# Tile start addresses of a one-core transformer block rearranged to multiples of 128 bytes in SBUF

## The chip, the cores and the metric

The program runs on one core of one Trainium2 chip. The metric is the device time of one execution in microseconds (us); several runs of each kernel are taken and the median is given. The profile is one further execution, recorded by the hardware profiler. The core's engines are TensorE (PE, with its weight loads listed apart as PEld), VectorE (DVE), ScalarE (ACT), GpSimd (POOL) and SyncE (SP, which issues the DMAs). All compute engines work on SBUF, 128 partitions of which each holds a row of every tile; a tile's start is a byte address that is the same in every partition. Matmul results go to PSUM.

## The reference, cut to what matters

The computation is one transformer block on 512 tokens of width 1024, in float32: a gated three-branch attention (compressed, selected and window keys) and a spatial gating unit side by side, then a feed-forward layer with a short convolution.

```
h = rms_norm(x, attn_norm);  proj = h @ w_in
q, kc, vc, ks, vs, kw, vw, gl, uv = split(proj)
o_nsa = nsa(q, compress(kc), compress(vc), ks, vs, kw, vw, sigmoid(gl), rel_bias)
o_sgu = u * (tril(sgu_w) @ rms_norm(v) + sgu_b)      # u, v = halves of gelu(uv)
x = x + concat([o_nsa, o_sgu]) @ w_out
up = rms_norm(x, ffn_norm) @ w_up                    # 1024 -> 2 * 2816
up = causal_conv3(up) + conv_b;  a, g = halves(up)
x = x + (silu(g) * a) @ w_down                       # 2816 -> 1024
```

## The kernel before, in words

**Precision.** Nearly every product is made of three matmuls. Each float32 operand is split into a high part in TensorE's float32r type and the remainder, also in float32r, and `mm3` (line 245) adds high by high, high by low and low by high into one PSUM bank. In `mm3` the argument `st` is the stationary operand (loaded as weights), `mv` the moving one that streams through:

```
TE.matmul(out, st[0], mv[0], start=first, stop=False)
TE.matmul(out, st[0], mv[1], start=False, stop=False)
TE.matmul(out, st[1], mv[0], start=False, stop=last)
```

**Stages.** The first projections (`wide`, `narrow`) keep the normalized input `ht_hi`, `ht_lo` stationary and move the weights, 512, 280 or 256 columns at a time. The remaining projections (`half`, five chunks, 480 matmuls of 256 columns, rows named `acc<-w_hi,ht_hi` and the like) run in between the attention steps (`scores`, `mix`), where `QT`, `KT`, `VT`, `PP`, `th` and `tl` are the operands. `w_out1` and `w_out2` multiply `w_out` (stationary) by `os` (the gating output) and `oa` (the attention output), 96 matmuls of 512 columns each. `up` (line 1275) makes the feed-forward's 44 column blocks of 128 features; each takes 24 matmuls of 512 columns (8 blocks of the width, three products), with the weights stationary and the normalized activations `h20`, `h21` moving (the trace calls both `h`): 1056 matmuls. `conv` (line 1300) then takes a finished block out of PSUM (line 1306, DVE), convolves it and gates it into `gA`, `gB` (high parts, blocks 0 to 7 and 8 to 21) and `gL` (low parts). `down` (line 1338) multiplies `w_down` by these in two halves of the output; in each half a weight tile again serves the equivalent of 24 matmuls of 512 columns; the second half splits one of its four outputs into two of 256 columns.

**Weights.** A weight tile of 512 KB is loaded by SP into one of three `w_raw` buffers, cast to `w_hi` (ACT or DVE) and subtracted to `w_lo` (DVE or POOL), three buffers each. The buffers are freed when PE is done with the tile, so in `up` and `down` the cast for the tile three ahead starts when a tile's last matmul ends.

**Order.** `Plan` runs all stages as threads against a table of costs and due times (`SLACK`, `BIAS`, `HEAD`, `STEPS`) and thereby fixes the order of the instructions on every engine before the program runs. Addresses are no part of that plan.

**Places in SBUF.** Tiles come from stacks of pools: `main` (kept throughout), `stream` (weight buffers), `att`, `uvp`, `sc`, `big` from the left, `s1`, later `s2`, `small` and `hp`, from the right. A pool places its tiles one behind the other as they are asked for, each rounded up to 32 bytes, so a tile of 16 bytes shifts whatever follows. A buffer that is placed where an older pool lay waits for the last readers of what it overlaps (`reuse_waits="tile"`). `PC` holds the compressed scores; `masks` (line 886) fills its masked columns on POOL. `rstd`, `r2` (four columns each), `qg` (one column), `vs` (four columns), `sm` (8 columns) and `ps` are the small tiles that lie between the wide ones.

## Time and profile before

| | |
|---|---|
| median of 3 runs | 635.57 us (634.92 to 636.78) |
| the profiled execution's own time | 635.98 us |
| its span, first to last instruction | 634.2 us |
| PE busy, share of the span | 620.6 us, 98% |
| DVE busy | 460.9 us, 73% |
| granted TensorE clock, mean | 1.000 |

The span is 1.8 us shorter than the execution's own time, which includes what lies around the instructions. A row of the timeline begins with the instruction's start in us from the start of the span and its duration in us; in brackets stands how long its engine was idle before it, and what ended that. PE's matmuls are pipelined: one starts before the one before it has ended, so the distance between two starts, not the duration, tells how fast they follow each other.

### The profile page before, as it was taken

The page shows a single profiled execution, that of the slowest core. Times are in us where ns is not written, and L with a number is a line of the kernel's source. Part 1 is how long each engine was busy: PE and PEld are TensorE (multiplying, and loading weights), DVE is VectorE, ACT ScalarE, POOL GpSimd, SP SyncE. Part 2 cuts the span into 40 slices and gives each one's busy share as a digit, 9 for nine tenths or more (in the row PEclk, how much of TensorE's full clock was granted, in tenths as well). Part 3 has the DMA queues.
Part 4 walks back from the last instruction along what each step waited for, and adds up shares of the span by engine and source line. Part 5 has one row for each costly group of instructions (what it writes and reads, how often), then busy time and mean ns, then how long its engine had stood idle before and what let it go on. Part 6 is the DMA issues. An engine that isn't in the chain of part 4 may idle for free.

```text
span 634.2 us, 8558 instructions
## 1 busy us (share of the span) xinstructions
PE 620.6 (98%) x3284; PEld 520.8 (82%) x3284; DVE 460.9 (73%) x788; ACT 231.5 (37%) x468; POOL 114.9 (18%) x109
## 2 busy tenths in 40 slices
PE   8999999999999999999999999999999999999998
PEld 5888988999997788888888888888888888888886
DVE  7778899989889666959877778877778853334331
ACT  5455477789888302334323132232222210000000
POOL 4139354111313001402101001010110100000000
PEclk9999999999999999999999999999999999999999
DMA  7836402102102421221222222222232222234201
GB/s 267 304 120 191 164 1 68 68 2 84 55 14 82 151 98 69 101 98 71 99 98 100 100 100 82 91 92 100 99 101 94 73 100 100 100 116 150 99 1 67
DMA packets 20805, 62.92 MB, mean 99 GB/s; under 512 B 2291, under 2 KB 3443, under 8 KB 20764
## 3 DMA queue, kind: packets, MB, share of 16 engines
q1 hardware_dynamic: 20620, 62.37, 28.7%
q8 instruction: 26, 0.43, 0.3%
q14 instruction: 15, 0.12, 0.1%
q10 hardware_dynamic: 144, 0.00, 0.0%
HBM read 60.24 MB, written 2.12 MB: 98 GB/s over the span
## 4 chain that ended last, share of the span: by engine, by line
PE 81%; DVE 10%; DMA 4%; ACT 2%; issue 1%; POOL 1%; SPq 0%; ACTq 0%; DVEq 0%; POOLq 0%
PE acc L246 11%; PE acc L248 11%; PE acc L247 11%; PE qk L248 9%; PE qk L247 8%; PE qk L246 8%; PE pv L1024 3%; PE tr L247 2%; PE tr L246 2%; PE tr L248 2%; PE pv L248 2%; PE pv L246 2%; PE pv L247 2%; PE qk L955 2%; PE tr L1005 2%; DMA x<-xp 2%
## 5 line engine op out<-in xcount | busy, mean ns | idle before, releaser
L232 DVE CAST w_hi<-w_raw 128x1024 fp32r<-128x1024 f32 (+2 forms) x84 | 56.6, 677 | 98.6 <-PE pv L247 27.6
L237 DVE TENSOR_TENSOR w_lo<-w_raw,w_hi 128x1024 fp32r<-128x1024 f32 (+3 forms) x93 | 123.7, 1332 | 5.3 <-ACT w_hi L231 3.0
L1312 ACT ACTIVATE cv<-up,col 128x512 f32<-128x512 f32 x44 | 35.9, 817 | 115.0 <-DVE up L1306 115.0
L248 PE MATMUL qk<-h,w_lo 128*128 128x512 f32 x176 | 70.2, 399 | 0.0
L248 PE MATMUL acc<-h,w_lo 128*128 128x512 f32 x176 | 70.2, 399 | 0.0
L247 PE MATMUL acc<-h,w_hi 128*128 128x512 f32 x176 | 69.4, 394 | 0.0
L247 PE MATMUL qk<-h,w_hi 128*128 128x512 f32 x176 | 69.3, 394 | 0.0
L246 PE MATMUL acc<-h,w_hi 128*128 128x512 f32 x176 | 69.2, 393 | 0.0
L246 PE MATMUL qk<-h,w_hi 128*128 128x512 f32 x176 | 69.0, 392 | 0.0
L246 PE MATMUL acc<-w_hi,ht_hi 128*128 128x256 f32 (+2 forms) x192 | 58.9, 307 | 0.0
L247 PE MATMUL acc<-w_lo,ht_hi 128*128 128x256 f32 (+2 forms) x192 | 55.7, 290 | 0.0
L248 PE MATMUL acc<-w_hi,ht_lo 128*128 128x256 f32 (+2 forms) x192 | 55.6, 290 | 0.0
L231 ACT ACTIVATE w_hi<-w_raw 128x1024 fp32r<-128x1024 f32 (+3 forms) x22 | 20.7, 942 | 76.7 <-PE pv L247 56.7
L238 POOL TENSOR_TENSOR w_lo<-w_raw,w_hi 128x1024 fp32r<-128x1024 f32 (+2 forms) x13 | 27.8, 2145 | 84.1 <-ACT w_hi L231 58.9
L238 POOL TENSOR_TENSOR gL<-cv,gB 128x512 fp32r<-128x512 f32 x13 | 18.7, 1435 | 126.9 <-ACT gB L231 126.9
L247 PEld LDWEIGHTS qk<-h,w_hi 128*128 128x128 f32 x176 | 33.0, 188 | 8.6
L247 PEld LDWEIGHTS acc<-h,w_hi 128*128 128x128 f32 x176 | 33.1, 188 | 8.5
L246 PEld LDWEIGHTS qk<-h,w_hi 128*128 128x128 f32 x176 | 33.0, 188 | 7.9
L246 PEld LDWEIGHTS acc<-h,w_hi 128*128 128x128 f32 x176 | 33.0, 188 | 7.8
L248 PEld LDWEIGHTS qk<-h,w_lo 128*128 128x128 f32 x176 | 33.0, 188 | 7.6
L248 PEld LDWEIGHTS acc<-h,w_lo 128*128 128x128 f32 x176 | 33.0, 188 | 7.6
L246 PEld LDWEIGHTS acc<-w_hi,ht_hi 128*128 128x128 f32 x192 | 36.2, 188 | 2.1 <-ACT xk L241 0.9
(300 smaller groups left out, 1427.5 us busy)
## 6 DMA issues: line engine op xcount, KB each, us to landing
w_raw<-wup SPq DMA_DIRECT2D x44, 512.0 KB, 3.2
w_raw<-wdn SPq DMA_DIRECT2D x22, 512.0 KB, 3.2
w_raw<-winH SPq DMA_DIRECT2D x11, 512.0 KB, 3.3
w_raw<-w SPq DMA_DIRECT2D x8, 512.0 KB, 4.6
w_raw<-wout SPq DMA_DIRECT2D x8, 512.0 KB, 3.2
bias<-bd SPq DMA_DIRECT2D x4, 528.0 KB, 7.4
x<-xp SPq DMA_DIRECT2D x1, 2048.0 KB, 10.6
xk<-xp SPq DMA_DIRECT2D x7, 256.0 KB, 4.0
```

The costliest lines, as they stand in the source:

```text
L231: return Pick("copy" + "ps"[sb], t, (ACT, act(n, 0) - 0.04 * (not sb), lambda: S.activation(dst, src, AF.Copy)), (DVE, d, lambda: V.tensor ...
L232: (DVE, d, lambda: V.tensor_copy(dst, src)))
L237: return Pick("both", t, (DVE, dve(n), lambda: V.tensor_tensor(dst, a, b, op)), (POOL, pool_cost(n), lambda: P.tensor_tensor(dst, a, b, op)))
L238: (POOL, pool_cost(n), lambda: P.tensor_tensor(dst, a, b, op)))
L246: TE.matmul(out, st[0], mv[0], start=first, stop=False)
L247: TE.matmul(out, st[0], mv[1], start=False, stop=False)
L248: TE.matmul(out, st[1], mv[0], start=False, stop=last)
L955: TE.matmul(s.tile[:, :L], QT[:, h, qs], KT[:, br - 1, g, l, :L], start=(l == 0), stop=(l == 1))
L1005: TE.transpose(ps.tile[:, r * 128:(r + 1) * 128], pp.tile[:, r, s * 128:s * 128 + 128], ident)
L1024: TE.matmul(o, v2.rearrange("p l d -> p (l d)"), x, start=(s == 0 and first and not l), stop=(s == nb - 1 and last and l == 1 and k == R - 1))
L1312: S.activation(c, u[:, 2:], AF.Identity, bias=C("cv", 4 * n + 3), scale=C("cv", 4 * n + 2))
```

## The change

Small tiles are asked for in other places and a filler of 96 bytes is added, so that the wide tiles behind them start at multiples of 128 bytes. No computation, no size of a wide tile and no line of the plan is changed. `rstd` and `r2` become two halves of one tile of 32 bytes ahead of `ht`; `qg` moves from `att` to `main`; the buffers of `th`, `tl`, `ot` and `of`, then `PC`, `ps`, the four `sm` buffers and `vs` (rounded up to 96 bytes) are asked for at once when `s2` is opened; `hp` gets a filler behind `sqn`.

```diff
+    rr = main.tile([128, 2, NT], F32, name="rr")
+    rstd, r2 = rr[:, 0], rr[:, 1]
+    qg = main.tile([128, 1], F32, name="qg")
     ht = (main.tile([128, KD, T], FR, name="ht_hi", tag="a16"), main.tile([128, KD, T], FR, name="ht_lo", tag="b16"))
...
-    rstd = main.tile([128, NT], F32, name="rstd")
-    qg = att.tile([128, 1], F32, name="qg")
...
         open_pool("small", side="right", reuse_waits="tile")
+        for r in (Rth, Rtl, Rot, Rof):
+            for n in range(r.bufs):
+                r.make(n)
+        box["PC"] = pools["s2"].tile([128, G, NT, R, 32], F32, name="PC")
+        box["ps"] = pools["s2"].tile([128, G, NT, R], F32, name="ps")
+        for n in range(Rsm.bufs):
+            Rsm.make(n)
+        box["vs"] = pools["s2"].tile([128, 8 + 16], F32, name="vs")[:, :NT]
         s2_ev.set(0.0)
...
     def masks():
         yield s2_ev
-        box["PC"] = pools["s2"].tile([128, G, NT, R, 32], F32, name="PC")
-        box["ps"] = pools["s2"].tile([128, G, NT, R], F32, name="ps")
...
-        vs = pools["s2"].tile([128, NT], F32, name="vs")
+        vs = box["vs"]
...
             box[n] = pools["hp"].tile([128, T], F32, name=n)
+        pools["hp"].tile([128, 24], F32, name="fill")
...
-        r2 = main.tile([128, NT], F32, name="r2")
```

In the two built programs the wide tiles start as follows; the remainder is that of the start address by 128.

| tile | remainder before | after | read by PE as |
|---|---|---|---|
| `ht_hi`, `ht_lo` | 64 | 0 | stationary |
| `os`, `gA` (same place as `ht_lo`) | 64 | 0 | moving |
| `x2` (same place as `ht_hi`) | 64 | 0 | not read |
| `eb`, `oa` | 32 | 0 | `oa` moving |
| `h20`, `h21` | 96 | 0 | moving |
| `RB`, `ssum`, `sqn` | 96 | 0 | `ssum` stationary |
| `th`, two buffers | 0 and 32 | 0 and 0 | moving |
| `tt0`, `tt1`, `PP`, `TTr`, `v_t` | 32 | 0 | stationary or moving |
| `PPs`, `u_t`, `ot`, `of`, `PC` | 64 | 0 | in part |
| `QT`, `KT`, `VT`, `bias`, `w_raw`, `w_hi`, `w_lo`, `tl`, `gB`, `gL`, `cv` | 0 | 0 | weights, `gB`, `gL`: both kinds |
| `xk` (32), `kn` (96), three of the four `up` tiles (32, 64, 96) | as given | the same | `kn` only |

Every engine issues the same instructions in the same order as before; two rows have other waits. On POOL, the fill of `PC` after the last `w_lo` of the first projections (names after MEMSET are what is filled; a name with _49 is a semaphore, by the engine or DMA queue that raises it). Before:

```order
L316 TENSOR_TENSOR kss<-kss,mhalf 128x4 [waits Pool_49]
L238 TENSOR_TENSOR w_lo<-w_raw,w_hi 128x560 [waits DMAHW6_49,DVE_49]
L893 MEMSET PC 128x4x24 [waits DMAHW4_49,DMAHW5_49,DVE_49,Activation_49]
L893 MEMSET PC 128x4x24
L893 MEMSET PC 128x4x16 x2
L893 MEMSET PC 128x4x8 x2
L315 TENSOR_SCALAR kcss<-kcss 32x2 [waits DVE_49]
```

and of the change:

```order
L318 TENSOR_TENSOR kss<-kss,mhalf 128x4 [waits Pool_49]
L238 TENSOR_TENSOR w_lo<-w_raw,w_hi 128x560 [waits DMAHW6_49,DVE_49]
L901 MEMSET PC 128x4x24 [waits DVE_49,PE_49,Activation_49]
L901 MEMSET PC 128x4x24
L901 MEMSET PC 128x4x16 x2
L901 MEMSET PC 128x4x8 x2
L317 TENSOR_SCALAR kcss<-kcss 32x2 [waits DVE_49]
```

`PC` lay where three `xk` buffers had been and now lies over the `ksq` and `kn` buffers, so its first fill no longer waits for two DMA queues and waits for PE instead, for the last transpose of `kn` (line 612 before). On ACT, the first square of the residual into `ssum`, ahead of `up`. Before:

```order
L231 ACTIVATE oa<-of 128x2x128 [waits DVE_49]
L231 ACTIVATE ot<-pv 64x512 [waits PE_49]
L241 ACTIVATE ssum<-x_2716 128x512 [waits DMAHW2_49,DVE_49,Activation_49]
L231 ACTIVATE w_hi<-w_raw 128x1024 [waits DMAHW5_49,PE_49,Pool_49]
L241 ACTIVATE sqn<-x_2716 128x512 [waits DVE_49]
```

and of the change:

```order
L231 ACTIVATE oa<-of 128x2x128 [waits DVE_49]
L231 ACTIVATE ot<-pv 64x512 [waits PE_49]
L241 ACTIVATE ssum<-x_2727 128x512 [waits DMAHW2_49,DVE_49]
L231 ACTIVATE w_hi<-w_raw 128x1024 [waits DMAHW5_49,PE_49,Pool_49]
L241 ACTIVATE sqn<-x_2727 128x512 [waits DVE_49]
```

It loses one wait, on ACT's own earlier work (`x_2716` and `x_2727` are both `x2`).

## Rows read from the trace of the kernel before

Times are us from the start of the span unless marked ns; `x` followed by a number is a count of instructions. A name such as `acc<-h,w_hi` lists what is written, then what is read.

**Rows 1.** The page, its fourth part: the chain that ended last, by engine.
```profile
PE 81%; DVE 10%; DMA 4%; ACT 2%; issue 1%; POOL 1%; SPq 0%; ACTq 0%; DVEq 0%; POOLq 0%
```

**Rows 2.** Stretches: 261 to 509 us; us, then busy PE, PEld, DVE, ACT, POOL, PEclk, DMA, GB/s.
```profile
261.00:509.00 248.00, 248.00 (x1073) 199.86 (x1072) 196.90 (x245) 69.98 (x95) 37.31 (x30) 1.00 0.27 96
```

**Rows 3.** Timeline of DVE in that stretch: start us, us, engine, line, what [idle before <-releaser].
```profile
380.95 0.69 DVE L1306 TENSOR_TENSOR up<-acc,RB 128x512 f32<-128x512 f32 x1
...
385.94 0.70 DVE L232 CAST w_hi<-w_raw 128x1024 fp32r<-128x1024 f32 x1 [1.22 <-PE qk L247]
386.55 0.69 DVE L1306 TENSOR_TENSOR up<-qk,RB 128x512 f32<-128x512 f32 x1
...
390.51 0.69 DVE L237 TENSOR_TENSOR cv<-cv 128x512 f32<-128x512 f32 x1 [0.70 <-ACT cv L1320]
391.54 0.70 DVE L232 CAST w_hi<-w_raw 128x1024 fp32r<-128x1024 f32 x1 [0.33 <-PE acc L247]
```

**Rows 4.** PE instructions that read h (h20, h21): ns min/median/max, first and last start.
```profile
L248 PE MATMUL qk<-h,w_lo x176: 394/399/399, 264.2 to 508.9; 128*128 128x512 f32 x176
```

**Rows 5.** Timeline of DVE in the down projection: weight splits, one for every 24 matmuls.
```profile
525.98 0.69 DVE L232 CAST w_hi<-w_raw 128x1024 fp32r<-128x1024 f32 x1 [3.60 <-PE pv L247]
...
531.61 0.69 DVE L232 CAST w_hi<-w_raw 128x1024 fp32r<-128x1024 f32 x1 [3.60 <-PE pv L247]
...
542.52 0.69 DVE L232 CAST w_hi<-w_raw 128x1024 fp32r<-128x1024 f32 x1 [3.42 <-PE pv L247]
...
547.96 0.69 DVE L232 CAST w_hi<-w_raw 128x1024 fp32r<-128x1024 f32 x1 [3.42 <-PE pv L247]
...
581.05 0.69 DVE L232 CAST w_hi<-w_raw 128x1024 fp32r<-128x1024 f32 x1 [3.58 <-PE tr L247]
...
586.66 0.69 DVE L232 CAST w_hi<-w_raw 128x1024 fp32r<-128x1024 f32 x1 [3.58 <-PE tr L247]
...
603.32 0.69 DVE L232 CAST w_hi<-w_raw 128x1024 fp32r<-128x1024 f32 x1 [3.52 <-PE tr L247]
...
608.86 0.69 DVE L232 CAST w_hi<-w_raw 128x1024 fp32r<-128x1024 f32 x1 [3.52 <-PE tr L247]
```

**Rows 6.** PE instructions that read gA, columns as in rows 4.
```profile
L246 PE MATMUL pv<-gA,w_hi x16: 397/398/398, 511.9 to 530.9; 128*128 128x512 f32 x16
```

**Rows 7.** PE instructions that read gB, columns as in rows 4.
```profile
L246 PE MATMUL pv<-gB,w_hi x28: 389/389/389, 534.4 to 569.1; 128*128 128x512 f32 x28
```

**Rows 8.** PE instructions that read os, columns as in rows 4.
```profile
L246 PE MATMUL acc<-os,w_hi x32: 393/394/483, 209.5 to 237.8; 128*128 128x512 f32 x32
```

**Rows 9.** Timeline of PE, 256-wide matmuls: eighteen, eighteen, twelve in a row, first and last.
```profile
95.23 0.28 PE L246 MATMUL acc<-w_hi,ht_hi 128*128 128x256 f32 x1
...
97.16 0.28 PE L248 MATMUL acc<-w_hi,ht_lo 128*128 128x256 f32 x1
...
174.52 0.28 PE L246 MATMUL acc<-w_hi,ht_hi 128*128 128x256 f32 x1
...
176.52 0.28 PE L248 MATMUL acc<-w_hi,ht_lo 128*128 128x256 f32 x1
...
601.81 0.28 PE L246 MATMUL qk<-gB,w_hi 128*128 128x256 f32 x1
...
603.12 0.28 PE L248 MATMUL tr<-gB,w_lo 128*128 128x256 f32 x1
```

**Rows 10.** Chain of waits from 73 to 205 us, shares by line.
```profile
by line: PE pv L1024 12.3%; PE qk L955 9.5%; DMA x<-xp 8.1%; PE acc L246 7.8%; PE tr L1005 7.8%; PE acc L248 7.5%; PE acc L247 7.5%; DVE QT L676 5.2%; DVE PPs L957 4.4%; DVE tl L1016 3.9%; DVE sm L970 2.8%; issue 2.5%; DVE QT L234 2.1%; PE 
```

**Rows 11.** POOL after the fill of PC (timeline), and the transposes of kn on PE.
```profile
72.44 0.18 POOL L315 TENSOR_SCALAR kcss<-kcss 32x2 f32<-32x2 f32 x1 [8.97 <-DVE kcss L815]
...
L612 PE MATMUL tr<-col,kn x16: 270/272/328, 50.6 to 63.0; 128*128 128x128 f32 x16
```

**Rows 12.** Timeline of PE with gA, the first matmul of two groups of three.
```profile
588.65 0.40 PE L246 MATMUL acc<-gA,w_hi 128*128 128x512 f32 x1
...
589.36 0.40 PE L246 MATMUL qk<-gA,w_hi 128*128 128x512 f32 x1
```
## The prediction

> **What bounds the kernel now.** I read the chain that ended last first. The reader is to see that PE holds 81% of it and DVE 10% [rows 1], so a gain has to come out of PE's rate or out of the waits between PE and DVE. The change adds and removes no work, so the question is whether the rate of any engine depends on where its tiles start. [...] That rate is read from DVE's timeline: the two reads of a finished block by line 1306 stand at 380.95 and 386.55, 5.60 us apart, and so do the weight casts at 385.94 and 391.54 [rows 3]. Every block is 24 matmuls of 512 columns, so one takes 5600 / 24 = 233.3 ns.

> The down projection does the same three products on the same sizes, and its weight casts mark 24 matmuls each too. While `gA` is read (remainder 64), they are 531.61 - 525.98 = 5.63 us apart; while `gB` is read (remainder 0), 547.96 - 542.52 = 5.44 us [rows 5], which is 226.7 ns for each matmul. `gL`, whose remainder is 0, is read in both. This is the comparison on which I rest the forecast: same lines of code, same weight buffers, same PSUM banks, same half of the output; what differs is which tile is moved through. It shows in single durations also: 397 to 398 ns with `gA` [rows 6], 389 for all 28 with `gB` [rows 7], a median of 399 with `h` at remainder 96 [rows 4] and 394 with `os` at remainder 64 [rows 8]. DVE's load does not explain it: in the down projection DVE stands idle 3.4 to 3.6 us before every cast on either side of the step [rows 5].

> **The change part by part.**

> *Up.* `h20` and `h21` go from remainder 96 to 0, as `gB` and `gL` have it; the weights are at 0 before and after. I take `gB`'s rate: 44 blocks x (5.60 - 5.44) = 7.0 us less, all on the path since PE is never idle there. What could be late next is DVE. In 11.20 us for two blocks it is idle 0.33 + 1.22 + 0.70 = 2.25 us [rows 3], so busy 8.95, and the new pace of two blocks is 10.88: it still follows, with 1.93 us to spare.

> *w_out.* `os` and `oa` are 96 matmuls each, 192 or eight times 24. The durations with `os` (394 ns) lie between 389 and the 399 of `h` [rows 4, 7, 8]; `oa`, at remainder 32, I put with them. I take the price of `up`: 8 x 0.16 = 1.3 us less, between nothing, if they were at `gB`'s rate already, and 8 x 0.19 = 1.5, if they are at `gA`'s.

> *Down.* In the first half four weight tiles meet `gA`: 4 x (5.63 - 5.44) = 0.76 us. In the second half, where one output in four is done in 256-column pieces, the casts stand 5.61 us apart with `gA` and 5.54 with `gB` [rows 5]: 4 x 0.07 = 0.28. Together 1.0 us less.

> *Matmuls of 256 columns.* Here the rows point the other way. The chunks of `half`, with the stationary `ht` at remainder 64, run at (176.52 - 174.52) / 17 = 117.6 ns; the 256-column pieces with everything at remainder 0 at (603.12 - 601.81) / 11 = 119.1 ns [rows 9]. There are 480 in `half`: 480 x 1.5 ns = 0.7 us more. Of their 480 x 0.1176 = 56.4 us, the chain of that stretch holds 7.8 + 7.5 + 7.5 = 22.8% of 132 us, 30.1 us or 53% [rows 10]; I count 0.4 us more. The bound from below is a faster stretch of the same line, (97.16 - 95.23) / 17 = 113.5 ns [rows 9]: 480 x 4.1 x 0.53 = 1.0 us less. I take the slower value, as that row alone has both operands at remainder 0.

> *The first projections* have 96 matmuls of 512 columns and 160 of 256 in a stretch paced by weight loads and splits. I cost them at nothing; without that cover they would give at most 96 x 6.7 ns = 0.6 us, and cost at most 160 x 1.5 ns = 0.2 us.

> *DVE, ACT and POOL operands.* The rows of line 1306 write tiles with different remainders (`up` at 0 or 32 and at 64 or 96, unchanged here) and both take 0.69 us [rows 3], so I cost their moves at nothing, either way. Lines that are on the chain in the attention stretch could shift by a few tens of nanoseconds; the range below holds that.

> *The wait on POOL.* The fill of `PC` now waits for the last transpose of `kn`, which starts at 63.0 [rows 11]. The fill ended before: POOL's next instruction, at 72.44, came after 8.97 us of idle time [rows 11], so the fill was over at 63.47. It moves by less than 1 us, into that idle time; behind it on POOL is only the instruction at 72.44, which waits for DVE. Cost nothing; if the idle time were gone, under 1 us. The wait that falls away on ACT was for ACT's own earlier work and costs nothing to lose.

> [...]

> The sum: -7.0 - 1.3 - 1.0 + 0.4 = -8.9 us. Against the profiled execution, 635.98 us with a span of 634.2, that is 627.1 us. That execution lies 0.4 us over the median of the runs, 635.57, so for a median I say **626.7 us**.

> **The rivals.**

> *Nothing changes: 635.6 us.* The 3% between `gA` and `gB`, and between `up` and `down`, could come from something that goes along with the stage: the layout of the weight tile or the neighbouring PSUM traffic. For it: `up` and `down` do have weight tiles of different layout, and the 256-column rows show that equal remainders need not mean an equal rate. Against it: `gA` and `gB` differ inside one stage, and `os`, with yet another layout, has the durations of `h`. [...]

> *Half of it: about 631.3 us.* The rate may depend on how the streams of moving data and weights fall together, of which the remainder is one part; the second half of the down projection is a sign, since 18 matmuls at 226.7 and 12 at 119.1 would be 5.51 us and 5.54 are seen [rows 5]. If `up`, `w_out` and `down` got half of what I count, -4.65 + 0.4 = -4.25 us.

> *Slower: about 640 us.* If the rate follows the interplay of the streams and not the start as such, the new places can lock into the worst pattern that the trace has: three matmuls in 589.36 - 588.65 = 0.71 us [rows 12], 24 in 5.68. In `up` that is 44 x 0.08 = 3.5 us more, in `w_out` 8 x 0.08 = 0.6, with the 0.4 us of the 256-column chunks 4.5 us more, 640.1. It decides at a block period in `up` of 5.60 us: below it the kernel gains, above it loses. Against it: in the rows with all operands at remainder 0 and 512 columns, 389 ns is the only duration [rows 7].

> **How the numbers follow.** My forecast has a chance of 0.78. Its own ends: 624.6 if the 256-column chunks take the faster value (1.4 us below the sum) and the first projections show their 0.6; 628.2 if those chunks cost the 0.7 and 0.2 us in full, `w_out` gives half and the second half of down nothing, -7.0 - 0.65 - 0.76 + 0.9 = -7.5. The half case has 0.1, nothing changed 0.07, slower 0.05. The range reaches from 624.6 up towards the half case, to 630.2. A measurement of this kernel can tell about 0.3%, 1.9 us, from no change: faster by more has 0.88 (forecast and half), within 0.07, slower 0.05.

> **What would show it.** Right: line 1306 in `up` stands 5.44 us apart instead of 5.60, and the durations with `h`, `os` and `gA` go to 389 ns; the casts of the down projection stand 5.44 apart from the first; the chunks of `half` go to 119 ns; POOL's fill of `PC` begins near 63.3 and its next instruction is no later than the shift of the rest; the stretch before 205 us is as long as it was to within about 1 us. Wrong: a block period at or near 5.60 in `up` with remainder 0, which would take the start address out of the explanation; or a period of 5.44 with new idle time on PE ahead of line 246, which would mean that DVE or the weight loads have become the bound.

## Result and profile after

The changed kernel takes 628.54 us (median of 6 runs, 627.55 to 630.74), the kernel before, run on the same occasion, 636.21 us (634.92 to 637.34): a ratio of 0.9883, 95% interval 0.9859 to 0.9906. The forecast was 626.7 us with a range of 624.6 to 630.2, so the measured time is 1.8 us above the forecast and inside the range. The sum of the prediction was made against one profiled execution: it said 627.1 us, and the profiled execution of the changed kernel took 627.58. Three of the six runs, at a mean granted clock of 1.000, took 627.55 to 627.72 us and the other three, at 0.997 and 0.994, 629.36 to 630.74, which is why the median lies above the profiled execution.

The page of the changed kernel, its head, two engines and the chain by engine:

```profile
span 625.9 us, 8557 instructions
...
PE 612.8 (98%) x3284; PEld 522.2 (83%) x3284; DVE 460.9 (74%) x788; ACT 231.9 (37%) x468; POOL 111.9 (18%) x109
...
PE 85%; DVE 9%; DMA 2%; ACT 1%; issue 1%; POOL 1%; SPq 0%; DVEq 0%; ACTq 0%; POOLq 0%
```

The instructions of PE, DVE, ACT and POOL are as many as before, and DVE's busy time is the same 460.9 us; PE is busy 7.8 us less and has a larger share of the chain [rows 1]. A view of 239 us of the up projection, the same stretch in the trace after and in the trace before, with the number of instructions in brackets:

```profile
261.00:500.00 239.00, 239.00 (x1063) 198.09 (x1063) 195.97 (x243) 69.59 (x95) 34.70 (x27) 1.00 0.29 97
```
```profile
261.00:500.00 239.00, 239.00 (x1034) 192.65 (x1033) 190.08 (x237) 67.74 (x92) 35.88 (x29) 1.00 0.27 95
```

PE is busy throughout at the same granted clock, 1.00, in both, but 1063 matmuls fall into the stretch instead of 1034, 2.8% more. The line that reads a finished block, now line 1314, and the cast that starts when a weight tile is done show the new pace on DVE's timeline:

```profile
382.17 0.69 DVE L232 CAST w_hi<-w_raw 128x1024 fp32r<-128x1024 f32 x1 [1.05 <-PE qk L247]
382.78 0.69 DVE L1314 TENSOR_TENSOR up<-qk,RB 128x512 f32<-128x512 f32 x1
...
387.61 0.69 DVE L232 CAST w_hi<-w_raw 128x1024 fp32r<-128x1024 f32 x1 [0.18 <-PE acc L247]
388.22 0.68 DVE L1314 TENSOR_TENSOR up<-acc,RB 128x512 f32<-128x512 f32 x1
```

388.22 - 382.78 = 5.44 us a block, where it was 5.60 [rows 3]. DVE still waits for PE before each cast, 1.05 and 0.18 us where it was 1.22 and 0.33, so it follows as the prediction had it. The casts of the down projection, the first four while `gA` is read, then two of the second half:

```profile
512.73 0.69 DVE L232 CAST w_hi<-w_raw 128x1024 fp32r<-128x1024 f32 x1 [3.12 <-PE pv L247]
...
518.17 0.69 DVE L232 CAST w_hi<-w_raw 128x1024 fp32r<-128x1024 f32 x1 [3.42 <-PE pv L247]
...
523.61 0.69 DVE L232 CAST w_hi<-w_raw 128x1024 fp32r<-128x1024 f32 x1 [3.42 <-PE pv L247]
...
529.05 0.69 DVE L232 CAST w_hi<-w_raw 128x1024 fp32r<-128x1024 f32 x1 [3.42 <-PE pv L247]
...
578.39 0.69 DVE L232 CAST w_hi<-w_raw 128x1024 fp32r<-128x1024 f32 x1 [3.52 <-PE tr L247]
...
583.93 0.69 DVE L232 CAST w_hi<-w_raw 128x1024 fp32r<-128x1024 f32 x1 [3.52 <-PE tr L247]
```

They are 5.44 us apart from the first and 5.54 in the second half, which [rows 5] had only with `gB`. Groups by tile, with min, median and max ns of one matmul, for `h`, `gA`, `os` and `oa`:

```profile
L248 PE MATMUL qk<-h,w_lo x176: 389/389/397, 263.8 to 501.7; 128*128 128x512 f32 x176
L246 PE MATMUL pv<-gA,w_hi x16: 389/389/389, 504.6 to 523.0; 128*128 128x512 f32 x16
L248 PE MATMUL acc<-os,w_lo x32: 387/389/400, 210.3 to 238.0; 128*128 128x512 f32 x32
L246 PE MATMUL tr<-oa,w_hi x8: 390/394/404, 249.4 to 257.1; 128*128 128x512 f32 x8
```

Line 248 with `h` falls from 399 to 389 [rows 4], `gA` from 398 [rows 6], `os` from 394 [rows 8]. **`oa` does not arrive**: it starts at a multiple of 128 like the others, and comes down only from a median of 397 to 394. The row of this group before the change:

```profile
L246 PE MATMUL tr<-oa,w_hi x8: 392/397/400, 249.7 to 257.5; 128*128 128x512 f32 x8
```

The next view is PE's timeline, the first and last of two runs of eighteen 256-column matmuls in the chunks of `half`:

```profile
95.06 0.28 PE L246 MATMUL acc<-w_hi,ht_hi 128*128 128x256 f32 x1
...
97.09 0.28 PE L248 MATMUL acc<-w_hi,ht_lo 128*128 128x256 f32 x1
...
174.68 0.28 PE L246 MATMUL acc<-w_hi,ht_hi 128*128 128x256 f32 x1
...
176.71 0.28 PE L248 MATMUL acc<-w_hi,ht_lo 128*128 128x256 f32 x1
```

Both run at 2.03 / 17 = 119.4 ns, where [rows 9] had 113.5 and 117.6 at these two places. On POOL the fill of `PC` starts at 63.19, behind the last transpose of `kn`, and the next instruction comes at 72.25 after 8.48 us of idle time [rows 11]: the new wait costs nothing.

```profile
63.19 0.59 POOL L901 MEMSET PC<- 128x96 f32 x6 [1.37 <-DVE KT L621]
72.25 0.18 POOL L317 TENSOR_SCALAR kcss<-kcss 32x2 f32<-32x2 f32 x1 [8.48 <-DVE kcss L817]
```

### The profile page after: what moved, and what is told of

The parts are those of the page before. It is cut to its first block, busy times and chain, and to the rows that moved or that the text cites. A ratio compares the mean times of both kernels' runs of the same rounds, so it can differ in the third digit from the quotient of the medians.

```text
span 625.9 us, 8557 instructions
## 1 busy us (share of the span) xinstructions
PE 612.8 (98%) x3284; PEld 522.2 (83%) x3284; DVE 460.9 (74%) x788; ACT 231.9 (37%) x468; POOL 111.9 (18%) x109
## 4 chain that ended last, share of the span: by engine, by line
PE 85%; DVE 9%; DMA 2%; ACT 1%; issue 1%; POOL 1%; SPq 0%; DVEq 0%; ACTq 0%; POOLq 0%
PE acc L246 12%; PE acc L247 12%; PE acc L248 12%; PE qk L246 9%; PE qk L247 9%; PE qk L248 9%; PE pv L1032 3%; PE pv L248 2%; PE pv L246 2%; PE pv L247 2%; PE qk L963 2%; PE tr L246 2%; PE tr L248 2%; PE tr L247 2%; PE tr L1013 2%; DMA x<-xp 2%
## 5 line engine op out<-in xcount | busy, mean ns | idle before, releaser
L246 PE MATMUL acc<-h,w_hi 128*128 128x512 f32 x176 | 68.7, 390 | 0.0
L248 PE MATMUL acc<-h,w_lo 128*128 128x512 f32 x176 | 68.5, 389 | 0.0
L247 PE MATMUL acc<-h,w_hi 128*128 128x512 f32 x176 | 68.5, 389 | 0.0
L248 PE MATMUL qk<-h,w_lo 128*128 128x512 f32 x176 | 68.5, 389 | 0.0
L238 POOL TENSOR_TENSOR gL<-cv,gB 128x512 fp32r<-128x512 f32 x13 | 16.9, 1296 | 124.6 <-ACT gB L231 124.6
```

The lines of the kernel that those rows point to most:

```text
L238: (POOL, pool_cost(n), lambda: P.tensor_tensor(dst, a, b, op)))
```

## Experiments

One row raised the question: `oa` is at a multiple of 128 and is not fast. Theory A is the prediction's: the moving tile's own remainder by 128 sets the pace. Theory B: the start of the moving tile and the start of the weight tile have to agree modulo 256. Theory C: the moving tile has to start at 128 modulo 256, wherever the weights lie. In the changed kernel `w_hi` and `w_lo` start at 128 modulo 256 (56448 bytes for the first buffer), as do `h20` (190336), `h21`, `os`, `gA`, `gB` and `gL`; `oa` (152064) starts at 0. The addresses are those of each compiled program.

The diffs are against the changed kernel unless said otherwise. In no experiment is a piece of the computation left out: where `rs` and `mhalf` are cut to 4 columns, unused columns go. Addresses are no part of the plan, so the order of the instructions stays as it was. Columns of the table: how many bytes `h20` lies behind the weight tile, modulo 256; the median time; the ratio to the kernel before with its 95% interval, where each ratio is to runs of the kernel before on the same occasion (their medians were 636.19 to 636.93 us), not to the first row; and up's 1056 matmuls, as the sum of the distances from each start to the next, and its mean. In up the granted clock was 1.00 before and after (261 to 500 us) and in e5, e10 and e12 (265 to 500 us); e1, e4, e8 and e9, at 0.997 over the whole span, have the same up as the changed kernel at 1.000 to within 0.1 us, so the last two columns compare like with like.

| kernel | h - w, bytes | us | ratio to before | up, us | ns |
|---|---|---|---|---|---|
| before | 96 | 636.21 | | 246.58 | 233.5 |
| after | 0 | 628.54 | 0.9883 [0.9859, 0.9906] | 239.68 | 227.0 |
| e1_oa | 0 | 628.56 | 0.9884 [0.9851, 0.9917] | 239.62 | 226.9 |
| e2_h2_plus128 | 128 | 635.18 | 0.9971 [0.9951, 0.9991] | 245.55 | 232.5 |
| e3_h2_undo | 96 | 635.72 | 0.9983 [0.9963, 1.0002] | 246.58 | 233.5 |
| e4_h2_only | 0 | 629.28 | 0.9892 [0.9867, 0.9917] | 239.64 | 226.9 |
| e5_left128 | 128 | 634.04 | 0.9958 [0.9943, 0.9973] | 245.56 | 232.5 |
| e6_left_h2 | 0 | 627.87 | 0.9860 [0.9827, 0.9893] | 239.68 | 227.0 |
| e7_h2_64 | 192 | 635.83 | 0.9990 [0.9973, 1.0006] | 246.58 | 233.5 |
| e8_ht128 | 0 | 628.48 | 0.9874 [0.9843, 0.9904] | 239.65 | 226.9 |
| e9_both32 | 0 | 628.86 | 0.9867 [0.9846, 0.9888] | 239.68 | 227.0 |
| e10_h2_32 | 224 | 636.03 | 0.9993 [0.9976, 1.0009] | 246.55 | 233.5 |
| e11_hi_only | 128 (`h21`: 0) | 630.89 | 0.9910 [0.9882, 0.9938] | 241.90 | 229.1 |
| e12_lo_only | 0 (`h21`: 128) | 633.69 | 0.9957 [0.9940, 0.9973] | 244.23 | 231.3 |

**Moving `oa` alone.** `gates` goes behind `eb`, so that `oa` starts at 151680, 128 modulo 256.

```diff
-    gates = att.tile([128, NT, 24], F32, name="gates")
...
+    gates = att.tile([128, NT, 24], F32, name="gates")
```

> The changed kernel, but gates (384 bytes) is placed behind eb and oa instead of ahead, so that oa moves from 152064 (0 modulo 256) to 151680 (128 modulo 256), where h20, h21, os, gA, gB, gL and all weight buffers stand; nothing else moves. Theory A, only the start modulo 128 of the moving tile matters: the 96 matmuls of oa keep their mean distance of 232.8 ns, and what kept them from 226.7 is the work beside them; the time stays within 0.3 us. Theory B, moving and weight tiles have to agree modulo 256: they go to about 226.7 to 228 ns and the kernel gains 96 x 6 ns = 0.5 us. Theory C, the moving tile has to stand at 128 modulo 256 whatever the weights do: the same as B here.

The group that had 390/394/404 after the change, now:

```profile
L246 PE MATMUL tr<-oa,w_hi x8: 389/389/389, 250.5 to 258.0; 128*128 128x512 f32 x8
```

`oa`'s 96 matmuls take 21.83 us instead of 22.34, the settled ones (95 of the 96) follow each other every 226.7 ns. Both places are multiples of 128, so A falls. The 0.5 us is less than the whole run can tell.

**Moving `h` by 128.** The filler grows from 24 to 56 columns; `h` starts at 0 modulo 256.

```diff
-        pools["hp"].tile([128, 24], F32, name="fill")
+        pools["hp"].tile([128, 56], F32, name="fill")
```

> The changed kernel with a filler of 224 bytes instead of 96 behind sqn: h20 and h21 move by 128 bytes, to 0 modulo 256, and stay at multiples of 128. Theory A: the blocks of up stay 5.44 us apart and the time is that of the changed kernel, 628.5. Theories B and C: up runs at the distance that oa has in the changed kernel, 232.8 ns, 24 of which are 5.59 us, and the kernel is 44 x 0.15 = 6.5 us slower, about 635.

`h` is again at a multiple of 128 and loses 5.87 of the 6.9 us. A falls a second time, on the longest stage; B and C stand.

**The filler taken away, and the filler alone.** e3 drops the line from the changed kernel; e4 puts it, alone, into the kernel before.

```diff
-        pools["hp"].tile([128, 24], F32, name="fill")
```

> The changed kernel without the filler: h20 and h21 back at remainder 96, all else as changed. If the filler of 96 bytes alone carries the gain in up: blocks 5.60 us apart again, 44 x 0.16 = 7.0 us slower than the changed kernel, about 635.5. If some other move (the buffers, the pools, the waits) carries it: no slower than 628.5 plus 1.

> The kernel before with the filler of 96 bytes as its only change: h20 and h21 at remainder 0, the waits and all other places as before. If the start of the moving tile in up is the cause: blocks 5.44 us apart, 7.0 us faster than before, and all that the rest of the change brings is under 1 us. If the rest carries it: blocks at 5.60 and the time of before, 636.2.

The one line has up's whole gain (239.64 us), and the rest of the change cannot be told from nothing in the whole run (0.9983, interval to 1.0002). In e4 `os` and `oa`, which it doesn't move, keep the pace of the kernel before: 233.3 ns for the 48 matmuls with `os` that run one behind the other, 234.3 ns for those with `oa`.

**Moving the weights instead of `h`.** Cutting `rs` and `mhalf` brings all tiles on the left 128 bytes lower, weights, `os`, `oa`, `gA`, `gB` and `gL` together; `h`, on the right, stays at 128 modulo 256. e6 then moves `h` after them, with the filler of 56.

```diff
-    rs = main.tile([128, 2, 16], F32, name="rs")
+    rs = main.tile([128, 2, 4], F32, name="rs")
...
-    mhalf = main.tile([128, 16], F32, name="mhalf")
+    mhalf = main.tile([128, 4], F32, name="mhalf")
```

> The changed kernel with rs and mhalf cut from 16 to 4 columns (only 4 of the 16 are ever computed with), which frees 128 bytes ahead of ht: all tiles placed from the left, the weight buffers, ht, os, gA, gB, gL, QT, KT, VT, oa among them, move down by 128 bytes; the tiles placed from the right, h20, h21, th, tl, stay. Weights then stand at 0 modulo 256, h20 and h21 at 128. Theory A, only the moving tile's start modulo 128: nothing changes, up 5.44 us a block, 628.5. Theory B, moving and weights have to agree modulo 256: up goes to about 5.59 us a block, 6.5 us slower; down, where both move, stays at 5.44. Theory C, the moving tile at 128 modulo 256: up stays at 5.44, but down (gB, gL now at 0) goes to about 5.59 us for 24 matmuls, 22 x 0.15 = 3.3 us slower, and oa (now at 128) gains 0.5.

> As the run with the left tiles 128 bytes lower, and h20, h21 128 bytes lower too, so that moving and weight tiles agree again, both at 0 modulo 256. Theory A: 628.5, up 5.44. Theory B: up and down both 5.44, 628.5. Theory C: up 5.59 and down 5.59, about 10 us slower. Together with the run before, this tells the difference of two starts from a single start.

DVE's timeline, two blocks of e5 and two of e6:

```profile
381.96 0.68 DVE L1314 TENSOR_TENSOR up<-acc,RB 128x512 f32<-128x512 f32 x1
...
387.53 0.69 DVE L1314 TENSOR_TENSOR up<-qk,RB 128x512 f32<-128x512 f32 x1
```
```profile
382.74 0.69 DVE L1314 TENSOR_TENSOR up<-qk,RB 128x512 f32<-128x512 f32 x1
...
388.18 0.68 DVE L1314 TENSOR_TENSOR up<-acc,RB 128x512 f32<-128x512 f32 x1
```

In e5 `h` has not moved and is slow, 5.57 us; `gA` and `gB` have moved to 0 modulo 256 together with their weights and are as fast as before the move (227.0 and 226.9 ns). `oa`, now at 128 modulo 256 but still 128 bytes off the weights, stays at 232.8 ns, where C had it gain. In e6 `h` is fast again at 0 modulo 256, 5.44 us. C falls, B holds: 245.56 us for up when the weights alone move, 239.68 when `h` moves with them, so what counts here is the pair.

**Other distances.** e7 has a filler of 40 columns, so `h` lies 64 bytes lower than after the change; e10 has one of 32, 32 bytes lower.

> The changed kernel with a filler of 160 bytes: h20, h21 at remainder 64 by 128 instead of 0 (96 before). If a multiple of 64 bytes is enough: up at 5.44 us a block. If it takes a multiple of 128: about 5.60 us, as os at 64 had 233 ns before, and about 7 us slower than the changed kernel.

> The kernel after the change with a filler of 32 columns in place of 24: h2 alone lies 32 bytes lower, all else stays. Theory B in its strict form (any difference modulo 256 costs the whole price): blocks of up at 5.58 to 5.60 us, the run 6 to 7 us above the kernel after, 635 us. A graded form (the price grows with the distance): 32 bytes of the 128 that are the most cost about a quarter, 1.5 us, the run at 630 us. If only 0 against 128 matters, 5.44 us and 628.5 us.

Two blocks of e10:

```profile
384.11 0.68 DVE L1314 TENSOR_TENSOR up<-acc,RB 128x512 f32<-128x512 f32 x1
...
389.71 0.68 DVE L1314 TENSOR_TENSOR up<-qk,RB 128x512 f32<-128x512 f32 x1
```

5.60 us, as before the change. 32 bytes off cost 6.87 us in up, 64 off 6.90, 128 off 5.87: no graded price. A filler of 32 columns is itself 128 bytes long; counting the filler's own size in multiples of 128 would have lost the whole gain.

**The other operands.** e8 cuts `rs` and `mhalf` and puts 128 bytes behind `ht`: `ht`, `os` and `gA` move to 0 modulo 256 and leave the weights, all else stays.

```diff
+    main.tile([128, 32], F32, name="pad")
```

> The changed kernel with rs and mhalf cut to 4 columns and a pad of 128 bytes behind ht: only ht_hi, ht_lo and what takes their places (os, gA, x2) move, to 0 modulo 256; weights and all else stay. In the projections ht is stationary and the weights move. Theory B: os and gA, moving against weights at 128, go to about 232 ns, 0.5 us and 0.7 us more; the matmuls of 256 columns in half, now with operands that disagree, leave 119 ns for 117.6 or less, up to 0.4 us back. Theory A: no change anywhere. Theory C: os and gA as in B, the 256-column ones unchanged.

```profile
L248 PE MATMUL acc<-os,w_lo x32: 390/393/404, 211.4 to 239.1; 128*128 128x512 f32 x32
L246 PE MATMUL pv<-gA,w_hi x16: 393/393/393, 505.7 to 524.2; 128*128 128x512 f32 x16
```

`os` and `gA` go slow as B says, 393 ns where the changed kernel has 389. In the first projections, where the weights move and `ht` is stationary, the 512-column matmuls go from 229.6 and 228.9 ns to 232.2 and 232.9, in the same direction, while the 256-column ones of `half` go from 119.1 to 118.7. What `os` and `gA` lose, 0.27 and 0.40 us, is about half of the 0.5 and 0.7 us that were expected, and too little to be told in the run's time. With `os` only the 48 matmuls that run one behind the other have a settled pace to lose (232.4 ns for 226.7). The matmuls with `gA` alternate with those of `gL`, which still agrees, and take 232.5 ns on line 246 but only 228.4 on line 248; e11 below shows the same pattern. The expected return of the 256-column matmuls to 117.6 ns or less did not come.

**All together by 32 bytes.** `mhalf` alone is cut and the filler is 32 columns: everything that up, down and `os` use lies at remainder 96 by 128, and agrees.

```diff
-    mhalf = main.tile([128, 16], F32, name="mhalf")
+    mhalf = main.tile([128, 4], F32, name="mhalf")
...
-        pools["hp"].tile([128, 24], F32, name="fill")
+        pools["hp"].tile([128, 32], F32, name="fill")
```

> The unused columns of mhalf are cut to 4 and the filler is 32 columns wide: all tiles on the left from th's pool neighbours on, the weight tiles, os, oa, gA, gB, gL and both h2 tiles lie 32 bytes lower together, so none is at a multiple of 128 any more, but h2, os, gA, gB and gL still agree with the weight tiles modulo 256. Theory B (what counts is that the moving tile and the weight tile agree modulo 256): blocks of up stay at 5.44 us, gA and gB at 227 ns, the run at 628.5 us (627 to 630). The rival that a multiple of 128 is needed besides the agreement: up at 5.57 us or more (5.8 us more in up) and the down projection at 232 ns for 462 matmuls of 512 columns (2.5 us more), the run at 636 us or more.

```profile
384.48 0.69 DVE L1314 TENSOR_TENSOR up<-qk,RB 128x512 f32<-128x512 f32 x1
...
389.92 0.68 DVE L1314 TENSOR_TENSOR up<-acc,RB 128x512 f32<-128x512 f32 x1
```

5.44 us, with none of these tiles at a multiple of 128. `h` here has the remainder 96 that it had in the kernel before, where a block took 5.60. None of these kernels can be told from the changed one as faster; moving `oa` is the only further gain that a trace shows, 0.5 us.

**One of the two `h` tiles.** e11 puts 128 bytes between `h20` (high part, moved by lines 246 and 248) and `h21` (low part, line 247), so `h20` disagrees; e12 also has the filler of 56, so that `h21` disagrees.

```diff
-        box["h2"] = [pools["hp"].tile([128, KD, T], FR, name=f"h2{n}") for n in range(2)]
+        box["h2"] = [pools["hp"].tile([128, KD, T], FR, name="h20")]
+        pools["hp"].tile([128, 32], F32, name="gap")
+        box["h2"].append(pools["hp"].tile([128, KD, T], FR, name="h21"))
```

> The kernel after the change with 128 bytes between h20 and h21: h20 (the high part, which two of three products of up move) is off the weights by 128 bytes, h21 agrees with them. If every matmul pays for its own pair of tiles: 704 of 1056 matmuls at 232.4 ns and 352 at 226.7, 3.9 us more in up, blocks at 5.53 us, the run at 632.4 us. If one tile that is off slows the whole stream: 5.9 us more, blocks at 5.57 us, 634.5 us or more. If only the low part's product pays: nothing, 628.5 us.

> The counterpart of e11_hi_only: the filler is 56 columns and 128 bytes lie between h20 and h21, so h21 (the low part, which one of three products of up moves) is off the weights by 128 bytes and h20 agrees with them. If a matmul pays only for its own pair of tiles, 352 of 1056 matmuls pay 5.7 ns, 2.0 us more in up (241.7 us), the run at 630.5 us. If, as in e11_hi_only, a matmul pays where it moves a tile that is off and the one behind it uses the same weight tile as it does, the low product (followed by one on the other weight tile) pays little: under 1 us more, 629 us. If any tile that is off slows all three products: 5.9 us more, 634.5 us.

Two blocks of e11, and two of e12:

```profile
385.19 0.69 DVE L1316 TENSOR_TENSOR up<-qk,RB 128x512 f32<-128x512 f32 x1
...
390.68 0.68 DVE L1316 TENSOR_TENSOR up<-acc,RB 128x512 f32<-128x512 f32 x1
```
```profile
381.45 0.68 DVE L1316 TENSOR_TENSOR up<-acc,RB 128x512 f32<-128x512 f32 x1
...
387.00 0.69 DVE L1316 TENSOR_TENSOR up<-qk,RB 128x512 f32<-128x512 f32 x1
```

**No expectation fits either.** With the tile off that serves two products in three, up loses 2.2 us (5.49 us a block); with the one that serves one in three, it loses 4.6 (5.55). By line, the mean distance to the next start is 227.3, 226.5 and 227.1 ns for lines 246, 247 and 248 after the change, 233.0, 225.9 and 228.4 in e11, and 231.4, 229.6 and 232.9 in e12. So a matmul whose own tiles agree can pay (lines 246 and 248 in e12), and one whose tiles don't can pay little (line 248 in e11). Nor does the price stay with a line: the kernel before and e3 both have `h` at a distance of 96 and both take 246.58 us for up, but the slow line is 248 in the kernel before (237.9 ns, the other two 231.1 and 231.4) and 246 in e3 (238.2, the other two 230.9 and 231.4). In these runs the price belongs to the sequence, not to single matmuls; what sets it stays open.

## Why the prediction was right, and where it was not

**What was right.** PE's rate in this kernel depends on where tiles start: one matmul of up took 233.5 ns before and 227.0 after. And PE bounds up (busy 239.00 of 239.00 us in both traces), `w_out` (50.50 of 51.00 us after, from 209 us on) and down (110.00 of 110.00 us after, from 502 us on), so a change with no change of work shortened the kernel. *Up*: 7.0 us were forecast; 246.58 - 239.68 = 6.9 came. *Down*: 1.0 forecast; the 512-column matmuls give 0.62 (`gA`) + 0.37 (`gL`) + 0.10 (`gB`), the 256-column ones with `gA` take 0.07 back, 1.0 in sum. *Chunks of `half`*: 119.1 ns instead of 117.4, their 480 distances add up to 61.69 us instead of 61.30, so 0.4 us, the forecast term, though how much of it lay on the path was not measured by itself. *First projections, DVE and POOL*: up begins at 260.6 us after and at 261.0 before. That shift holds all stages before up, `w_out`'s 0.5 us and `half`'s 0.4 us included, so nothing is left for these terms beyond a few tenths. The spans give the same sum: 634.2 - 625.9 = 8.3 us, of which 0.4 fall before up, 6.9 in it and 1.0 behind it.

**The step that failed** is *w_out*: "I take the price of `up`: 8 x 0.16 = 1.3 us less". 0.55 us came, 22.91 - 22.51 = 0.40 with `os` and 22.49 - 22.34 = 0.15 with `oa`. Two reasons, both in the trace. `oa` lies 128 bytes off the weights, modulo 256, and goes from 234.3 ns only to 232.8; moving it recovers 0.5 us. And of the 96 matmuls with `os` only the last 48 run one behind the other (233.3 to 226.7 ns, 0.3 us); the first 48 mostly come in groups of six between other matmuls, of which the first takes about 315 ns in both kernels and most of the others 224 to 236 without a settled pace.

**What else moved the number.** The prediction went from a profiled execution to a median by taking off 0.4 us. In the changed kernel the profiled execution, 627.58 us, lies 0.96 us below the median. Of the 1.8 us between 626.7 and 628.54, that step makes 1.4 and the parts of the sum 0.5, `w_out` above all. So 628.54 lies above the upper end of the forecast's own terms and is in the range because the range was drawn on towards the half case. Those ends add up to 624.7 and 628.1, where the prediction has 624.6 and 628.2. Two durations were also read from single groups: the 399 ns with `h` [rows 4] are line 248, while lines 246 and 247 have medians of 392 to 394 in the same trace, and 389 ns is "the only duration" in the group of [rows 7], while another with `gB` (line 246, into `acc`) reaches 396. Neither enters the sum.

**The rule behind it was half wrong.** The step "as `gB` and `gL` have it; the weights are at 0 before and after" took the remainder by 128 of the moving tile as what counts. The comparison of `gA` with `gB` was sound, but it also varied the distance to the weight tile, and that distance, modulo 256, is what the experiments single out: 239.6 to 239.7 us for up in the six kernels with both `h` tiles at 0, 245.5 to 246.6 in the six with both at 96, 128, 192 or 224. That the forecast came near was in this respect luck: `h`, `gA` and `os` happened to land on the weights' half of the 256 bytes, and `oa` did not. Had the filler been 128 bytes longer, every tile would have kept its multiple of 128 and the time would have been 635.18 us (e2), where the same reasoning says 626.7.

**The rivals.** *Nothing changes* falls with the first view: up runs at 5.44 us a block, not 5.60. *Half of it* named what e5 and e6 single out, "how the streams of moving data and weights fall together", but not its price, as the change happened to bring nearly all pairs together. *Slower* did not occur: in no kernel here does up run slower than in the kernel before, 5.60 us a block.

**What stays open.** With `h` left where it is, moving the weights by 128 bytes costs 5.88 us in up (e5), and e6, which moves `h` after them, gets it back. No run shows how the two tiles are read, so why the distance counts is not known from this case.

## What to carry to other kernels

Where TensorE bounds a stage, compare the distance between matmul starts across tiles that differ in where they lie: 226.7 against 233 ns for 512 columns was a gain of 2.8% in that stage, and one filler line brought it. For streams like these (float32r, 512 columns; no other was seen to gain here) compare the address of the moving tile with that of the weight tile it meets, modulo 256, not with a round number (up took 5.44 us a block at a distance of 0, 5.57 to 5.60 at 96, 128, 192 and 224), and after the change read one row for each such tile: the one that stayed slow (`oa`) led to the rule. Two rows that differ prove only that something differs between them, so list what else does before a rule is made of it.
